# The MLP's second map for both token blocks at once: 26 block products added up in PSUM, with the sums for them made beside the first map

## The chip, the cores and the metric

The kernel runs on one core of a Trainium2 chip. The metric is the device time of one execution in microseconds (us), from the first instruction to the last. Engines named below: TensorE (PE, matmuls; PEld is its weight load), VectorE (DVE), ScalarE (ACT), GpSimd (POOL) and SyncE (SP). Here POOL does little besides issuing DMAs, and SP nothing else. SBUF is the on-chip memory of 128 partitions, PSUM the accumulator that TensorE writes: 8 banks of 128x512 floats. DRAM tiles are scratch outside the core.

## The reference

One layer over S = 2048 tokens of width D = 1024 in float32, with a conditioning vector that gives shift, scale and gate to each of two sub-layers. Cut to what matters:

```
mod = silu(c) @ w_ada + b_ada ; sh1, sc1, g1, sh2, sc2, g2 = split(mod)

h = x * (1 + sc1) + sh1 ; z = h @ w_in                    # 1024 -> 2048
mix = concat(gated conv of width 3, multi-scale pooling) @ w_out
x = LayerNorm(alpha * x + (1 + g1) * mix)

h = x * (1 + sc2) + sh2
f = square(relu(h @ w_mlp_in)) @ w_mlp_out                # 1024 -> 4096 -> 1024
x = LayerNorm(alpha * x + (1 + g2) * f)
```

The two matmuls of the last part, the first map (1024 to 4096) and the second map (4096 to 1024), are most of the arithmetic. Call U = square(relu(..)), 2048 x 4096, the first map's output, and W the second map's weights, 4096 x 1024.

## The kernel before, in words

*Precision.* TensorE multiplies a rounded float32 form at full speed. Each operand of a product is split in two: ScalarE casts it to a high part, VectorE subtracts that from the operand for a low part (`split`, L87 to L89; `parts` calls it for weights). A product is three matmuls, high times high, high times low, low times high (`mm3`, L92 to L95), so each operand tile of 128x1024 costs one cast on ScalarE and one subtraction on VectorE before TensorE may use it.

*Block products.* The tokens are two blocks b of T = 1024. The FF width is cut into NC = 8 column groups g of 512. Each matrix product is a 2x2 by 2x2 product in the form of Strassen and Winograd: 7 block products in place of 8, on sums of quarter blocks of each factor. Sums are VectorE adds (`tt`, L97), made once and kept in DRAM where more than one use needs them.

*Order of the stages.* For each token block: input projection, convolution and pooling, output projection, LayerNorm and transposes into blocks of the first map's token operand (`turned` with `back`; four sums pass through the DRAM tile `hsave`, L811), the first map, the second map, LayerNorm and store (`Close`). The first map, `up(b, g, B)` (L991), runs its 7 products for each g, 24 matmuls of 128x512 each, 56 products for a block; ScalarE does relu and square; VectorE makes sums of quarter blocks of U; POOL stores 8 tiles of 512 KB for each g in `usum` (`save`, L1012). Operand "4" of `back` is the last that column group 0 needs.

The weights' sums for the first map are made by `block_weights` (L518) as each g comes, or read back from `w1sum` for g below 2. The weights' sums for the second map are made by `sum_blocks` (L960) beside the first map of block 0: for each g and column half four loads of 256 KB on SP (L965), four adds of 128x512 and four stores on POOL (L971) to `w2sum`, with two fresh tiles each time.

The second map, `down(b, F, g2, close)` (L1116), runs once for each block. It has 7 products in 2 halves of 4 column groups; operands of the next half are loaded and split while this one is multiplied. Results are added from PSUM into eight row tiles F. In block 1 one of the seven products is cut once more (`DEEPER`, `deep_operands`, `deep_matmuls`, `deep_sums`): 7 products of quarter size, 8 x 7 x 6 = 336 matmuls of 128x256 in place of two halves of full size; its sums come from `sum_deep` (L974) and `closed` (L1062). `sum_x`, the gate's part of `ada` and `row_by_dram` (which turns the gate to a row) run beside the second map of block 0, as do `residual` (alpha times x in 8 rows) and `close.turn()`, which prepares the input projection of block 1.

*What sets the order.* The Python code names the work; a scheduler at build time lays the instructions of each engine down in one fixed order and hands out the slots of the tile pools: 28 tiles h, 10 o, 6 w, 5 r of 128x1024 floats, and 8 PSUM banks. An engine takes its instructions in that order and waits at each for its data and its tile. DMAs issued by SP and POOL stand in these engines' order too.

Of the kernel before, what the change touches and what calls it, by code (L numbers as in the profile page):

```python
# [13 lines left out]
P = 128  # L14
D = 1024
# [16 lines left out]
DEEPER = (1,)  # L32

DIRECT = 12
DEEP_SUMS = (0,), (1,), (2,), (3,), (4, 5), (6, 7), (), ()
HALF_SUMS = (1, 2, 3, 3, 3, 3, 3, 0)
# [14 lines left out]
def tile_hybrid_layer(ctx: ExitStack, tc: tile.TileContext, opening, xT, x, wada, win,  # L51
# [129 lines left out]
    w2sum = tc.dram_tile([NC, 4, P, T], F32, name="w2sum")  # L181
    usum = tc.dram_tile([NC, 8, P, T], F32, name="usum")
    hsave = tc.dram_tile([4, P, T], F32, name="hsave")
    nsave = tc.dram_tile([8, P, D], F32, name="nsave")
    rsave = tc.dram_tile([8, P, D], F32, name="rsave")
    gout = tc.dram_tile([2, KD // 2, P, T], F32, name="gout")
    winsum = tc.dram_tile([4, P, T], F32, name="winsum")
    w1sum = tc.dram_tile([2, 4, P, T], F32, name="w1sum")
# [4 lines left out]
    udeep = tc.dram_tile([NC, P, 3 * Q], F32, name="udeep")  # L193
    wdeep = tc.dram_tile([NC, P, T + 3 * Q], F32, name="wdeep")
# [323 lines left out]
    def block_weights(src):  # L518
        a11, a12, a21, a22 = [t_r() for _ in range(4)]
        for i, r in enumerate((a11, a12, a21, a22)):  # L520
            nc.sync.dma_start(r, src[i])
        yield a11
        yield a12
        s1 = t_r()
        tt(s1, a21, a22, ALU.add)
        tt(a21, a11, a21, ALU.subtract)
        tt(a11, s1, a11, ALU.subtract)
        tt(a12, a12, a11, ALU.subtract)
        for r in (a11, s1, a21, a12, a22):
            yield r  # L530
# [58 lines left out]
    def sum_x(k, after):  # L589
        ab = []  # L590
        for i in (k, k + 4):
            r = t_o()
            nc.sync.dma_start(r, xT[i])
            with tc.issue_after(after[0]):
                nc.scalar.activation(r, r, AF.Identity, bias=mod[:, 2 * i + SH1 : 2 * i + SH1 + 1],
                                     scale=mod[:, 2 * i + SC1 : 2 * i + SC1 + 1])
            ab += [r[:, :H], r[:, H:], r]
        b11, b12, b1, b21, b22, b2 = ab
        with tc.issue_after(after[1]):
            tt(b12, b12, b11, ALU.subtract)  # L600
# [265 lines left out]
    def out_proj(b, ops):  # L866
# [35 lines left out]
        def scale():  # L902
            t = late.pop()
            begun[:] = [nc.vector.tensor_scalar(R[t], R[t], mv[t][:, 0:1], mv[t][:, 6:7], op0=ALU.add,
                                                op1=ALU.mult).ins]
            nc.gpsimd.dma_start(nsave[t], R[t])
# [67 lines left out]
    def sum_deep(g):  # L974
        a, e = t_o(T), t_o(T)
        nc.sync.dma_start(a, w2[g, 2])
        b11, b12, b21, b22 = (a[:, i * Q : i * Q + Q] for i in range(4))
        t2, t3, t4 = (e[:, i * Q : i * Q + Q] for i in range(3))
        tt(t3, b22, b12, ALU.subtract)
        tt(b12, b12, b11, ALU.subtract)  # L980
        tt(t2, b22, b12, ALU.subtract)
        tt(t4, b21, t2, ALU.subtract)
        nc.gpsimd.dma_start(wdeep[g][:, :T], a)
        nc.gpsimd.dma_start(wdeep[g][:, T:], e[:, : 3 * Q])

# [3 lines left out]
    left = []  # L989

    def up(b, g, B):  # L991
        X, Y, Z = {}, {}, {}
        order = (0, 1, 5, 4, 6, 7, 3) if g else (0, 1, 7, 4, 5, 6, 3)
        product = seven(summed_weights(w1[g], w1sum[g], order) if g < 2 else block_weights(w1[g]), B)
        ps = [slice(p * H, p * H + H) for p in range(2)]

# [10 lines left out]
        def join(r, banks):  # L1007
            add(r, banks)
            nc.scalar.activation(r, r, AF.Relu)
            nc.scalar.activation(r, r, AF.Square)  # L1010

        def save(r, i):  # L1012
            nc.gpsimd.dma_start(usum[g, i], r)  # L1013

        product(0, X, True)
        c11 = keep(X)
        product(1, Y, True)
        join(c11, Y)
        save(c11, 0)
# [13 lines left out]
        else:  # L1033
            product(3, Z, True)
            c22 = keep(Z)
        product(4, X, False)
        join(c22, X)
        save(c22, 3)
# [5 lines left out]
        s1 = t_o()  # L1044
        tt(s1, c12, c22, ALU.add)
        tt(c12, c11, c12, ALU.subtract)
        tt(c11, s1, c11, ALU.subtract)
        for i, r in ((4, s1), (6, c12), (5, c11)):
            save(r, i)
# [5 lines left out]
        if b not in DEEPER:  # L1055
            tt(c11, c21, c11, ALU.subtract)
            save(c11, 7)
            save(c21, 1)
            return


        def closed(s4):  # L1062
            tt(s4, c21, c11, ALU.subtract)
            save(s4, 7)
            e = t_o()
            a11, a21, a12, a22 = (c21[:, i * Q : i * Q + Q] for i in range(4))
            q1, q2, q4 = (e[:, i * Q : i * Q + Q] for i in range(3))
            tt(q1, a21, a22, ALU.add)
            tt(q2, q1, a11, ALU.subtract)
            tt(a21, a11, a21, ALU.subtract)  # L1070
            tt(q4, a12, q2, ALU.subtract)
            save(c21, 1)
            nc.gpsimd.dma_start(udeep[g], e[:, : 3 * Q])

        if g + 1 < NC:
            closed(c11)
        else:
            left.append(closed)


    def down_operands(i, gs, scale=None):
        a, w = ORDER[i]
        out_ = []
        for g in gs:
            r = t_r()
            nc.sync.dma_start(r, usum[g, 3 + int(a[1]) if a[0] == "s" else 2 * int(a[0]) + int(a[1]) - 3])
            q = t_w(F32)
            nc.sync.dma_start(q, w2sum[g, int(w) - 1] if len(w) == 1 else w2[g, 2 * int(w[0]) + int(w[1]) - 3])
            if scale is not None:
                for hs in halves:  # L1090
                    tt(q[:, hs], q[:, hs], scale, ALU.mult)
            pair = []
            for src in (r, q):
                hi, lo = t_h(), t_h()
                done = split(src, hi, lo)
                pair += [hi, lo]
            out_.append(pair)
        return out_, done

    def residual():  # L1100
        ag, ab = row(t_o(D), rows[0]), row(t_o(D), rows[1])
        after = yield
        with tc.issue_after(after[0]):
            nc.scalar.mul(ag, ag, ALPHA)
        nc.scalar.mul(ab, ab, ALPHA)
        for t in range(8):
# [8 lines left out]

    def down(b, F, g2, close):  # L1116
        X, Y = {}, {}
        lo_, hi_ = halves
        closing = b + 1 == NB
        deeper = b in DEEPER  # L1120
        steps = [(i, hf) for i in ((1, 0) if deeper else (0, 1)) + (2, 3, 5, 4, 6) for hf in range(2)]

        def operands(n):
            i, hf = steps[n]
            return down_operands(i, range(4 * hf, 4 * hf + 4), g2[:, lo_] if closing and n + 1 == len(steps) else None)


        def matmuls(banks, ops, new, begins, ends, then, by_tile):
            if new and begins:
                for t in range(4):  # L1130
                    banks[t] = t_ps()
            every = range(len(ops))
            for t, n in ([(t, n) for t in range(4) for n in every] if by_tile else
                         [(t, n) for n in every for t in range(4)]):
                uh, ul, wh, wl = ops[n]
                for p in range(2):
                    cs = slice(p * H + t * P, p * H + t * P + P)
                    ws_ = halves[p]
                    mm3(banks[t], uh[:, cs], ul[:, cs], wh[:, ws_], wl[:, ws_],
                        new and begins and n == p == 0, ends and n == len(ops) - 1 and p == 1, not new)  # L1140
                if ends and n == len(ops) - 1:
                    then(t, banks[t])

        def keep(t, cs, ps):
            nc.scalar.copy(F[t][:, cs], ps)

        def add(t, cs, ps):
            tt(F[t][:, cs], F[t][:, cs], ps, ALU.add)

        def gate(t, cs):  # L1150
            tt(F[t][:, cs], F[t][:, cs], g2[:, cs], ALU.mult)

        def first_row(t, ps):
            add(t, hi_, ps)
            r = t_r()
            nc.sync.dma_start(r, rsave[t])
            gate(t, slice(0, D))
            for hs in halves:
                close.add(t, hs, r[:, hs])
            close.normalise(t)  # L1160


        def saved(hs):
            out_ = []
            for i in range(2):
                r = t_r()
                nc.sync.dma_start(r.rearrange("p (a n) -> p a n", a=2),
                                  rsave[4 + 2 * i : 6 + 2 * i, :, hs].rearrange("a p n -> p a n"))
# [3 lines left out]
        rest = {}  # L1172

        def second_row(t, ps):
            add(t + 4, hi_, ps)
            gate(t + 4, hi_)
            close.add(t + 4, hi_, rest[4][t])
            close.first_half(t + 4, 1)

        def last(t, ps):  # L1180
            tt(F[t + 4][:, lo_], ps, g2[:, lo_], ALU.mult)
            close.add(t + 4, lo_, rest[6][t])
            close.normalise(t + 4)

        def gated_first(t, ps):
            tt(F[t + 4][:, lo_], ps, g2[:, lo_], ALU.mult)
            tt(F[t + 4][:, lo_], F[t + 4][:, lo_], rest[6][t], ALU.add)

        def last_half(ops):
            for t in range(4):
# [306 lines left out]
```

## Time and profile before

The kernel took 1735.1 us, the median of 3 runs (1734.13 to 1736.8). The profile is that of one execution on the one core.

| | |
|---|---|
| median of runs | 1735.1 us |
| profiled execution, first to last instruction (its span) | 1733.2 us; its time is recorded by this span |
| TensorE busy | 1723.5 us, 99%, 7855 instructions |
| VectorE busy | 1314.6 us, 76%, 1726 instructions |
| ScalarE busy | 868.1 us, 50% |
| GpSimd busy | 205.8 us, 12% |
| DMA | 465.24 MB, mean 268 GB/s |

How such a profile is read: the busy line gives each engine's busy time, its share of the span and the number of its instructions. The slices cut the span into 40 equal parts, one digit each, in tenths. The chain that ended last is followed back from the last instruction, at each step to what released it; its shares say which engine or transfer the time lies on. A group line gives line, engine, operation, output and inputs with their shapes, count, then busy time and mean nanoseconds of one, then the idle time of the engine before them and what ended it. A source view of a DMA line gives the durations of the issuing instruction, the first and last start, and the time from issue to landing (least, median, most). A window row gives, for a stretch, the busy time of each engine with its instruction count, the granted clock of TensorE, the share of the DMA engines, and GB/s.

### The profile page before, as it was taken

What the parts mean: (1) busy time and instruction counts of PE and PEld (TensorE: products, weight loads), DVE (VectorE), ACT (ScalarE), POOL (GpSimd) and SP (SyncE); (2) the same over time, 40 slices, a digit from 0 to 9 for tenths busy, and PEclk for the clock granted to TensorE, in tenths of its full rate; (3) what the DMA queues carried; (4) which work ended last, traced back from release to release, by engine and by line L of the source; (5) the groups of instructions that cost most, each with busy time, mean ns of one, the idle gap of its engine ahead of it and who ended that gap; (6) DMA issues with size and microseconds to landing.
All of it is one profiled execution on the core that took longest, in us unless ns stands there. A gap on an engine that the chain in (4) does not pass through costs nothing.

```text
span 1733.2 us, 21912 instructions
## 1 busy us (share of the span) xinstructions
PE 1723.5 (99%) x7855; PEld 1435.5 (83%) x7855; DVE 1314.6 (76%) x1726; ACT 868.1 (50%) x1172; POOL 205.8 (12%) x399
## 2 busy tenths in 40 slices
PE   9999999999999999999999999999999999999998
PEld 7888888888888888888888888888888889888887
DVE  8897798877777686669686789687566778665896
ACT  6323368554445554446573344775444567444451
POOL 0222220122322000100000000102111110000000
PEclk9999999999999999999999999999999999999999
DMA  9998877778888998887572366657545589777771
GB/s 387 345 337 319 302 267 269 267 262 325 311 326 319 381 418 332 291 286 284 196 271 76 110 219 219 230 185 282 215 179 222 197 290 418 294 273 249 267 264 50
DMA packets 142685, 465.24 MB, mean 268 GB/s; under 512 B 16488, under 2 KB 17008, under 8 KB 142576
## 3 DMA queue, kind: packets, MB, share of 16 engines
q1 hardware_dynamic: 97920, 303.39, 48.0%
q0 software_dynamic: 44656, 160.46, 24.4%
q8 instruction: 61, 1.00, 0.2%
q14 instruction: 48, 0.39, 0.1%
HBM read 318.55 MB, written 145.23 MB: 268 GB/s over the span
## 4 chain that ended last, share of the span: by engine, by line
PE 95%; DMA 3%; issue 1%; DVE 1%; ACT 0%; SPq 0%; POOL 0%; DVEq 0%; POOLq 0%
PE ps L95 30%; PE ps L93 30%; PE ps L94 30%; PE ps L425 3%; DMA r<-in_w 1%; DMA usum<-o 1%; PE ps L773 1%; DVE o L98 0%; DMA o<-in_w 0%; DMA o<-in_opening 0%; DVE w L89 0%; DVE r L98 0%; ACT w L88 0%; DVE o L1369 0%; SPq L108 0%
## 5 line engine op out<-in xcount | busy, mean ns | idle before, releaser
L95 PE MATMUL ps<-h,w 128*128 128x512 f32 x1312 | 510.2, 389 | 0.4 <-DVE w L89 0.4
L94 PE MATMUL ps<-h,w 128*128 128x512 f32 x1312 | 510.3, 389 | 0.0
L93 PE MATMUL ps<-h,w 128*128 128x512 f32 x1312 | 510.0, 389 | 0.0
L93 PE MATMUL ps<-h,h 128*128 128x512 f32 (+1 forms) x1176 | 444.2, 378 | 0.0
L95 PE MATMUL ps<-h,h 128*128 128x512 f32 (+1 forms) x1176 | 444.1, 378 | 0.0
L94 PE MATMUL ps<-h,h 128*128 128x512 f32 (+1 forms) x1176 | 444.0, 378 | 0.0
L88 ACT CAST h<-r 128x1024 fp32r<-128x1024 f32 (+2 forms) x186 | 187.8, 1014 | 298.0 <-PE ps L94 186.8
L95 PEld LDWEIGHTS ps<-h,w 128*128 128x128 f32 x1312 | 246.3, 188 | 52.1 <-DVE w L89 0.8
L94 PEld LDWEIGHTS ps<-h,w 128*128 128x128 f32 x1312 | 246.3, 188 | 51.5 <-DVE h L89 0.5
L93 PEld LDWEIGHTS ps<-h,w 128*128 128x128 f32 x1312 | 246.0, 188 | 51.3 <-ACT h L88 0.2
L89 DVE TENSOR_TENSOR h<-r,h 128x1024 fp32r<-128x1024 f32 (+2 forms) x186 | 217.3, 1173 | 93.5 <-ACT h L88 93.0
L88 ACT CAST w<-r 128x1024 fp32r<-128x1024 f32 x156 | 164.3, 1053 | 242.6 <-PE ps L94 231.3
L89 DVE TENSOR_TENSOR w<-r,w 128x1024 fp32r<-128x1024 f32 x156 | 190.5, 1222 | 96.3 <-ACT w L88 95.4
L94 PEld LDWEIGHTS ps<-h,h 128*128 128x128 f32 x1176 | 221.3, 188 | 41.1
L95 PEld LDWEIGHTS ps<-h,h 128*128 128x128 f32 x1176 | 221.3, 188 | 40.8
L93 PEld LDWEIGHTS ps<-h,h 128*128 128x128 f32 x1176 | 221.3, 188 | 40.5
L98 DVE TENSOR_TENSOR o<-o,o 128x1024 f32<-128x1024 f32 (+2 forms) x193 | 171.1, 890 | 41.0 <-DMA usum<-o 31.8
L98 DVE TENSOR_TENSOR o<-o,ps 128x512 f32<-128x512 f32 (+1 forms) x175 | 113.7, 658 | 54.3 <-PE ps L95 53.4
L89 DVE TENSOR_TENSOR h<-w,h 128x1024 fp32r<-128x1024 f32 x114 | 137.6, 1207 | 4.3 <-ACT h L88 4.1
L88 ACT CAST h<-w 128x1024 fp32r<-128x1024 f32 x114 | 118.6, 1040 | 12.8 <-DMA w<-wdeep 4.1
L1013 POOL DMA_DIRECT2D usum<-o x111 | 59.4, 535 | 472.3 <-ACT o L1010 195.0
L98 DVE TENSOR_TENSOR r<-r,r 128x1024 f32<-128x1024 f32 x60 | 73.4, 1223 | 21.5 <-DMA r<-in_w 17.5
(160 smaller groups left out, 1243.0 us busy)
## 6 DMA issues: line engine op xcount, KB each, us to landing
usum<-o POOLq DMA_DIRECT2D x111, 512.0 KB, 4.8
r<-usum SPq DMA_DIRECT2D x109, 512.0 KB, 5.5
w<-w2sum SPq DMA_DIRECT2D x64, 512.0 KB, 5.9
r<-in_w SPq DMA_DIRECT2D x60, 512.0 KB, 6.0
w<-in_w SPq DMA_DIRECT2D x40, 512.0 KB, 7.4
o<-in_w SPq DMA_DIRECT2D x72, 256.0 KB, 6.4
w2sum<-o POOLq DMA_DIRECT2D x64, 256.0 KB, 6.7
msum<-o POOLq DMA_DIRECT2D x18, 512.0 KB, 4.9
```

The lines of the kernel that those rows point to most:

```text
L88: high = nc.scalar.copy(hi, src)
L89: return high.ins, nc.vector.tensor_tensor(lo, src, hi.bitcast(F32), op=ALU.subtract).ins
L93: nc.tensor.matmul(ps, whi, xhi, start=first, stop=False, skip_group_check=goes_on)
L94: nc.tensor.matmul(ps, whi, xlo, start=False, stop=False, skip_group_check=goes_on)
L95: nc.tensor.matmul(ps, wlo, xhi, start=False, stop=last, skip_group_check=goes_on)
L98: return nc.vector.tensor_tensor(out_, a, b_, op=op)
L425: nc.tensor.matmul(ps[m, h], wt[:, w : w + P], A[k][p // 2][:, hs], start=k == 0 and p == 0, stop=k == KD - 1 and p == 2)
L773: nc.tensor.transpose(ps[:, t * P : t * P + P], R[4 * h + t][:, k * P : k * P + P], ident)
L1013: nc.gpsimd.dma_start(usum[g, i], r)
```

## The change

The second maps of both token blocks become one stage behind both first maps. U is cut 4 by 4 (rows: each part holds a quarter of either block, 512 tokens together; columns: each part gathers 128 columns of every column group, 1024 together), W 4 by 2, and their product is formed from 26 block products (`PRODUCTS`), where the form of 7 for 2x2 by 2x2 would give 28. An entry of `PRODUCTS` names the sum of U, the sum of W, a sign, whether it starts a fresh set of PSUM banks, and which parts of the result read the banks behind it, with which factor. The products go by turns to two sets of 4 banks; one that is not fresh adds onto what its set already holds, so that sums of products are formed in PSUM. There are 8 fresh starts and 30 reads of a set into the 16 row tiles F. The stage is a stream of 26 x 4 units of 24 matmuls of 128x512, with operands loaded and split 4 units ahead. A negative sign is put into the split (in `operand`).

`up` makes 33 sums of 128x256 for each g and block in four stages (`U_SUMS`), and stores 26 tiles of 128 KB on POOL. `sum_down` makes the sums of W: for each of 8 column groups 13 loads, 20 adds of 128x512 (`W_SUMS`) and 17 stores, in four registers (halves of two tiles). It is a generator, drawn on by `beside()` at seven places of each column group of the first map (four in group 0): first the gate's part of `ada`, then 6 sums of W for each `sum_x`, the gate's row and the sums of the input weights, then 2 sums of W at each place, on through the first map of block 1. `block_weights` stores the first map's weight sums in block 0 for all g, and block 1 reads them back. `prepare` runs after the first map of block 0. `Close` serves 16 rows at once, and the output is stored by SP. The quarter-size stage and its sums are gone.

The diff, cut to its core (the tables of `U_SUMS`, `W_SUMS` and `PRODUCTS` with their first rows):

```diff
-DEEPER = (1,)
...
+SLOTS = 26
+RAW_SLOT = (0, 4)
+U_SUMS = (
+    ((1, 5, -1, 1, 16), (0, 1, 1, 2, 1), (16, 0, 1, 3, 19)),
...
+W_SUMS = (
+    (3, 6),
+    (2, 7),
+    (1, 3, 2, -1, 8),
+    (0, 4),
+    (2, 0, 3, -1, 9),
+    (0, 2),
+    (3, 0, 3, -1, 10),
+    (3, 1, 0, -1, 11),
...
+PRODUCTS = (
+    (13, 2, 1, True, ((3, 0, 1), (3, 1, 1))),
+    (2, 3, 1, True, ((0, 1, 1),)),
+    (15, 11, 1, False, ((3, 1, -1),)),
...
-    def block_weights(src):
+    def block_weights(src, dst=None):
...
+        if dst is not None:
+            for i, r in enumerate((s1, a11, a21, a12)):
+                nc.gpsimd.dma_start(dst[i], r)
...
-    def up(b, g, B):
+    def up(b, g, B, beside):
...
+        def stored(slot, z):
+            nc.gpsimd.dma_start(usum[slot, g // 2, :, b, g % 2, :], z)
+
+        def sums(stage):
+            if stage == 0:
+                stored(RAW_SLOT[0], parts_[RAW_SLOT[1]])
+            for x, y, sign, slot, at in U_SUMS[stage]:
...
+                z = parts_[at]
+                tt(z, where[x], where[y], ALU.add if sign > 0 else ALU.subtract)
...
+                if slot >= 0:
+                    stored(slot, z)
...
+    def sum_down():
+        for g in range(NC):
+            tiles = [t_o() for _ in range(2)]
+            regs = [r[:, hs] for r in tiles for hs in halves]
+            for step in W_SUMS:
+                if len(step) == 2:
+                    to, i = step
+                    src = w2[i, g // 2] if i < 8 else wsum[i - 8, g // 2]
+                    nc.sync.dma_start(regs[to], src[:, halves[g % 2]])
+                    continue
+                yield
+                to, x, y, sign, i = step
+                tt(regs[to], regs[x], regs[y], ALU.add if sign > 0 else ALU.subtract)
+                if i >= 0:
+                    nc.gpsimd.dma_start(wsum[i - 8, g // 2][:, halves[g % 2]], regs[to])
...
+    def down(g2, close):
...
+        def operand(n, gp):
+            s, w, sign = PRODUCTS[n][:3]
+            r = t_r()
+            nc.sync.dma_start(r, usum[s, gp].rearrange("p b g n -> p (b g n)"))
+            q = t_w(F32)
+            nc.sync.dma_start(q, w2[w, gp] if w < 8 else wsum[w - 8, gp])
...
+            hi, lo = t_h(), t_h()
+            if sign > 0:
+                split(r, hi, lo)
+            else:
+                nc.scalar.mul(hi, r, -1.0)
+                nc.vector.scalar_tensor_tensor(lo, r, -1.0, hi.bitcast(F32), op0=ALU.mult, op1=ALU.subtract)
+            return hi, lo, *parts(q)
...
+        stream = [(n, gp) for n in range(last + 1) for gp in range(4)]
+        ready = [operand(*x) for x in stream[:4]]
...
+            if k + 4 < len(stream):
+                ready.append(operand(*stream[k + 4]))
+            ops = ready.pop(0)
+            _, _, _, new, reads = PRODUCTS[n]
+            if gp == 0:
+                if new:
+                    banks[n % 2] = [t_ps() for _ in range(4)]
...
+            for i in range(4):
+                unit(banks[n % 2][i], i, ops, new and gp == 0, gp == 3, not new)
+            if gp == 3:
+                for t, d, c in reads:
+                    read(t, d, c, banks[n % 2])
...
-                store = nc.gpsimd if b + 1 < NB else nc.sync
-                store.dma_start(out[b * T + t * P : b * T + t * P + P, cs], z[:, cs])
+                nc.sync.dma_start(out[t * P : t * P + P, cs], z[:, cs])
...
+    def first_side():
+        for n in range(0, 8, 2):
+            ada(G2 + n, G2 + n + 2, nc.sync.dma_start, lambda: t_o(D))
+            yield
+        weights = sums_down
+        for n in range(4):
+            for _ in range(3):
+                next(weights)
+                next(weights)
+                yield
+            sum_x(n)
+            yield
...
+    def second_side():
+        for _ in sums_down:
+            next(sums_down, None)
+            yield
...
     for b in range(NB):
         B, back = out_proj(b, in_proj_1(*ready) if b else in_proj_0())
-        ready, gate = mlp(b, B, back, gate)
+        first_map(b, B, back)
+        if b == 0:
+            ready = prepare()
+    for _ in sums_down:
+        pass
+    close = Close()
+    down(gate[0], close)
```

494 lines of the change are left out of this document (200 added, 294 removed), and 3 rows, old and new, of the table U_SUMS.

## The prediction

> **What bounds the kernel now.** I read the page first: busy times, slices, and the chain that ended last.
>
> ```profile
> span 1733.2 us, 21912 instructions
> ...
> PE 1723.5 (99%) x7855; PEld 1435.5 (83%) x7855; DVE 1314.6 (76%) x1726; ACT 868.1 (50%) x1172; POOL 205.8 (12%) x399
> ...
> PE   9999999999999999999999999999999999999998
> ...
> PEclk9999999999999999999999999999999999999999
> ...
> PE 95%; DMA 3%; issue 1%; DVE 1%; ACT 0%; SPq 0%; POOL 0%; DVEq 0%; POOLq 0%
> ```
>
> TensorE is busy 99% of the span and is 95% of the chain: the kernel ends when its matmuls are done. So matmuls taken out pay at full price, and anything new that makes TensorE wait also does. The second view is the table of windows: a stretch of the first map of block 0, both first maps nearly whole, and the stage of quarter-size products that opens the second map of block 1.
>
> ```profile
> core 0: us, PE busy (x) PEld busy (x) DVE busy (x) ACT busy (x) POOL busy (x), PEclk, DMA share, GB/s
> 300.00:345.40 45.40, 45.40 (x201) 37.23 (x200) 38.15 (x40) 26.23 (x31) 5.89 (x11) 1.00 0.74 265
> 275.00:560.00 285.00, 284.57 (x1272) 235.44 (x1271) 221.35 (x249) 149.44 (x183) 67.09 (x125) 1.00 0.80 296
> 1121.00:1425.00 304.00, 304.00 (x1362) 252.00 (x1361) 217.08 (x255) 166.87 (x204) 42.31 (x79) 1.00 0.62 225
> 1424.31:1464.58 40.27, 40.27 (x337) 40.25 (x336) 33.27 (x37) 27.79 (x33) 2.67 (x5) 1.00 1.02 408
> ```
>
> Row one gives the pitch: 45.40/200 = 0.227 us a matmul of 512 columns, so a product of 24 takes 5.45. Rows two and three show how full the first maps are: VectorE 221 of 285 and 217 of 304, with TensorE full. VectorE's slack there, 64 and 87 us, is what the change draws on.
>
> **The change, part by part.** *Matmuls.* Before, the second map has 13 full block products of 8 groups times 24 matmuls (2496) and the quarter-size stage of 336 narrow ones. After, it has 26 products over 4 units of 24: 2496 again. So exactly the quarter-size stage goes, 40.27 us by row four: **−40.3**.
>
> *Durations for what is added* (VectorE, ScalarE and POOL groups by shape; busy time and mean ns stand behind the count):
>
> ```profile
> L89 DVE TENSOR_TENSOR w<-r,w 128x1024 fp32r<-128x1024 f32 x156 | 190.5, 1222 | 96.3 <-ACT w L88 95.4
> L98 DVE TENSOR_TENSOR o<-o 128x512 f32<-128x512 f32 x64 | 42.9, 686 | 4.7 <-DMA o<-gout 4.5
> L98 DVE TENSOR_TENSOR o<-o 128x256 f32<-128x256 f32 x40 | 15.9, 419 | 1.1 <-DMA o<-in_w 0.6 <-ACT o L1054 0.3
> L88 ACT CAST w<-r 128x1024 fp32r<-128x1024 f32 x156 | 164.3, 1053 | 242.6 <-PE ps L94 231.3 <-DMA o<-gout 4.7 <-DMA r<-in_wins 3.4
> ...
> L1013 POOL DMA_DIRECT2D usum<-o x111 | 59.4, 535 | 472.3 <-ACT o L1010 195.0 <-DVE o L98 176.8 <-DVE r L98 53.7
> ```
>
> *U sums.* Each column group and block makes 33 sums of 256 columns, 13.8 us by 0.419 (264 in block 0, 111 us), where it had 4 of 1024 columns (32×1.22 = 39): 72 us more for VectorE, which had 64 free. Stores to usum go from 111 to 416, 305×0.535 = 163 us more issue on POOL over two first maps; POOL was busy 67 of 285, so that fits.
>
> *W sums.* In place of 64 sums over four independent registers a half come 8 column groups of 20 sums of 512 columns, 13 loads (SP) and 17 stores (POOL), all in four half-tiles that are used again and again. A register may be loaded again only when its store has landed, and summed only when its load has landed. Followed sum by sum, 10 loads and 9 stores of a group stand one behind the other. With l and s for their times to landing, a group takes C = 10 l + 9 s + 20×0.685 (13.7). The source views of the like transfers of 256 KB, of 512 KB stores before that stage, and of the block loads:
>
> ```profile
> L965 SPq DMA_DIRECT2D o<-in_w x64: 327/424/1590, 320.7 to 545.9; - x64
> ...
> DMA to landing us min/median/max: 2.8/6.4/8.8
> ```
> ```profile
> L971 POOL DMA_DIRECT2D w2sum<-o x64: 542/542/552, 329.6 to 557.6; - x64
> ...
> DMA to landing us min/median/max: 3.6/6.5/9.1
> ```
> ```profile
> L545 POOL DMA_DIRECT2D w1sum<-w x8: 542/547/547, 241.5 to 255.8; - x8
> ...
> DMA to landing us min/median/max: 2.3/7.1/9.5
> ```
> ```profile
> L811 SPq DMA_DIRECT2D o<-hsave x4: 382/402/427, 308.0 to 1154.7; - x4
> ...
> DMA to landing us min/median/max: 4.2/5.2/7.0
> ```
>
> So l lies between 2.8 and 6.4 and s between 2.3 and 6.5. C is 28+21+13.7 = 62 at least and 64+58+13.7 = 136 at most.
>
> *Where the first group stands: a hole.* In the built order, the 20 sums of column group 0 are a nearly solid run on VectorE, right in front of the subtractions whose output is operand "4" of column group 0. These subtractions read blocks loaded back from hsave; those loads stand on SP behind the run's weight loads, and take the tile slots that the run frees. TensorE needs operand "4" for the last product of column group 0, after 10 products and the transposes of that map. So TensorE stops there, about 327 us into the span (the map begins near 269), until the run is through, and all behind the run on VectorE and SP waits with it. The run cannot start early: its second sum stands behind a split whose tile is freed by the product just before the stop. The stop is: cast and split 1.05+1.22; 10 loads and 9 stores; 19×0.685 = 13.0; the last store; the hsave load; sum, cast and split again (3.5). Little else is under way in a stop, so I take both l and s at 3.3, between the shortest seen and the medians and near the shortest: 2.3+62.7+13.0+3.3+4.2+3.5 = **+89**. At the shortest values 2.3+28+20.7+13+2.3+4.2+3.5 = 74; at the medians, with hsave 5.2, 153.
>
> By the Trainium skill ("DMA: Bandwidth & Descriptors", Anatomy of one DMA — SWDGE (gpsimd) path) such a transfer costs about 2.0 us plus its bytes over 436e3, an estimate of 2.6 us for 256 KB; the stop would be 2.3+49.4+13+2.6+4.2+3.5 = 75, and a group 63. The rows agree at their minimum, not at their median of 6.4.
>
> *Just behind the stop* VectorE has 67.5 us of its own work to 60 of TensorE's: **+6** (0 to 15).
>
> *Groups 1 to 3, first map of block 0.* They lie over the next 34 products, 185 us. Each starts when the one before has made 15, then 12, of its 20 sums, so they take 1+14/19+12/19 = 2.37 C. VectorE is in order: where a sum waits, the splits behind it wait too, and TensorE has operands for a few products only. VectorE's other work there is 58×1.22+42×0.685+177×0.42 = 174 us, which fills the waits in part; I take a quarter, 44, as not fitting. Transfers overlap with those of the stage, so l and s are halfway between shortest and median, 4.6 and 4.4: C = 46+39.6+13.7 = 99. 2.37×99+44 = 279, against 185: **+94**. From 0 (C = 62: 192, all but hidden) to 182 (C = 136).
>
> That such waits reach TensorE's chain at all is seen in the map before, where a loaded sum, a store and a reload stand in a row (the chain around 450 us; start, us, what):
>
> ```profile
> 444.14 9.05 DMA r<-in_w
> ...
> 459.35 0.54 POOL usum L1013
> 459.89 4.38 issue
> 464.28 3.85 DMA usum<-o
> 468.16 0.70 DVE o L98
> ...
> 508.21 7.72 DMA o<-in_w
> 515.98 1.86 DVE o L98 x3
> ```
>
> *Groups 5 to 7, first map of block 1*: 35.5 products, 193 us; 2.26 C; other VectorE work 137, a quarter 34. 2.26×99+34 = 258: **+65** (0 to 148).
>
> *Group 4* runs over from one block into the next, beside the input projection: **+5** (0 to 30).
>
> *Second map.* 26×96×0.227 = 567 us, operands asked for 4 units (21.8 us) ahead against 6.4 for a load; sums go from PSUM into F beside it, and VectorE, with two splits of 1.22 to each unit of 5.45 and 30 reads of 4 banks (82 us at 0.685), has a third of its time left. The out stores move from POOL to SP, in front of operand loads that have that lead. **0** (−15 to +15); with the lead gone, each late unit would cost its load, 6. *Moved work* (ada for the gate, xsum, the gate's row) goes into the first map of block 0: about 21 us of VectorE, counted in the 174 above. The stored w1 sums save 24 sums of 1.22 in block 1, which is in the 137. The residual and the input projection's preparation are the same work at another place: nothing, beside a full TensorE.
>
> *Sum.* 1735.1 − 40.3 + 89 + 6 + 94 + 65 + 5 = **1954**. All durations are from an execution of span 1733.2, 1.9 below the median, which I leave in. Ends: 1735.1−40.3+74−15 = 1754 and 1735.1−40.3+153+15+182+148+30+15 = 2238.
>
> **The rivals.**
> *Only the stop.* The later groups hide behind TensorE, if transfers land near their shortest time: 1735.1−40.3+89+6 = **1790**. For it: C = 62 gives 192 against 185. Against: in the loaded map the median load was 6.4.
>
> *The matmuls slow down after stalls.* In the start-up, small matmuls between waits are longer than the same in the filled stage:
>
> ```profile
> L127 PE MATMUL ps<-o 128*128 128x128 f32 x10 | 2.5, 437 | 1.1 <-DVE o L129 1.1
> L773 PE MATMUL ps<-ident,o 128*128 128x128 f32 x128 | 15.6, 275 | 0.0
> ```
>
> 437/275 = 1.59. If stalls brought that back all through the paced stages, they would be limited by TensorE itself: 34×5.45×1.59 = 295 for 279 and 35.5×5.45×1.59 = 308 for 258: 1954+66 = **2020**. Against: the clock row has no slice below 9, but also no long gap in it. By the Trainium skill ("TensorE: Matmul & The Clock Gate", Part 1: The HAM clock gate) the clock halves after an idle window of about 3.4 us and needs about as long busy to come back; products at twice their time would make 371 and 387, and 2175. No run so far shows such a gap.
>
> *The other side: faster.* The stop doesn't hold TensorE, and the groups pass behind it: 1735.1−40.3 = **1695**. The one mechanism is the run of group 0 being through before TensorE needs operand "4". It decides when the stop is under 40.3 us, that is (40.3−2.3−13.0−4.2−3.5)/20 = 0.9 us for each of the 20 transfers in its sum, or when the run begins 49 us sooner. The shortest transfer seen is 2.3.
>
> **How the numbers follow.** The forecast 0.60, with its own range 1840 to 2060 (a C of about 80 to 115 for both maps); only the stop 0.20; slow matmuls 0.10; faster 0.08; within 0.2%, which is what a measurement here can tell from no change, 0.02. Slower is thus 0.90. The range has to take in the stop alone (1790) and reach past the slow matmuls, and so runs from 1780 to 2150; the case of 1695, and what lies above, are left out.
>
> **What would show it.** A gap of TensorE of some 90 us from about 327 us on, ended by VectorE behind a load of hsave; in it, stores to wsum and loads of in_w of 256 KB by turns, and VectorE's waits put down to them. The first maps, 56 products or 305 us of matmuls each, at about 305+89+6+94 and 305+65. A second map of about 567 us with TensorE full, and no narrow matmuls at its start. If the granted clock falls below 1.00 around the gaps, the slow-matmul rival is right. The prediction is wrong if VectorE's waits in the later groups are short (transfers near 3 us, or groups that overlap more than 2.37 C says), or if the second map is short of operands.

## The result and the profile after

The changed kernel took 1978.6 us (median of 4 runs, 1976.97 to 1987.07) beside 1735.95 for the kernel before (median of 4): a ratio of 1.1407, interval 1.1383 to 1.1432. It is 14% slower. The forecast was 1954, with a range of 1780 to 2150.

The page of the changed kernel (span; busy line; slices of TensorE, VectorE and the granted clock; the chain that ended last):

```profile
span 1975.1 us, 22593 instructions
...
PE 1741.5 (88%) x7519; PEld 1422.8 (72%) x7519; DVE 1422.5 (72%) x2222; ACT 839.7 (43%) x1148; POOL 402.2 (20%) x767
...
PE   9999986218968875899998889789999999999998
...
DVE  7987867327767676688967667667666487686998
...
PEclk9999997659988988999999898989999999999999
...
PE 41%; issue 11%; DMA 11%; DVE 6%; POOL 3%; ACT 1%; DVEq 0%; SPq 0%; POOLq 0%; ACTq 0%
```

TensorE's work was to shrink by 40 us, yet its busy time rose from 1723.5 to 1741.5, and it now idles 234 us. The holes in its row begin in the sixth slice (from 247 us) and end with the 27th (1333 us); behind it the row is full. The clock row, without a digit below 9 before, goes down to 5 where TensorE stands still, and to 8 in many slices behind.

The windows table, cut at the first matmul of each stage, says where the time went. First the changed kernel: first map of block 0, input and output projection of block 1, first map of block 1, the joint second map.

```profile
core 0: us, PE busy (x) PEld busy (x) DVE busy (x) ACT busy (x) POOL busy (x), PEclk, DMA share, GB/s
269.70:762.50 492.80, 340.38 (x1379) 271.10 (x1379) 308.53 (x526) 181.72 (x233) 159.01 (x298) 0.83 0.66 223
762.50:1025.80 263.30, 236.87 (x1042) 194.21 (x1041) 207.50 (x294) 119.61 (x176) 39.10 (x70) 0.95 0.60 210
1025.80:1399.50 373.70, 329.69 (x1378) 265.84 (x1377) 249.44 (x451) 166.64 (x213) 132.37 (x248) 0.93 0.69 225
1399.50:1967.40 567.90, 566.49 (x2521) 469.65 (x2519) 425.22 (x537) 254.95 (x348) 16.84 (x32) 1.00 0.72 252
```

The same stages of the kernel before; here the second map of block 0 stands second and that of block 1 last:

```profile
269.40:578.60 309.20, 308.77 (x1378) 255.50 (x1377) 235.40 (x272) 165.72 (x213) 68.17 (x127) 1.00 0.81 299
578.60:883.30 304.70, 304.70 (x1346) 252.25 (x1345) 221.94 (x262) 161.02 (x207) 15.48 (x29) 1.00 0.82 305
883.30:1115.60 232.30, 232.29 (x1041) 192.48 (x1040) 182.22 (x250) 114.96 (x180) 17.80 (x30) 1.00 0.50 178
1115.60:1424.20 308.60, 308.60 (x1379) 255.66 (x1378) 220.98 (x267) 171.56 (x219) 42.34 (x79) 1.00 0.62 226
1424.20:1725.70 301.50, 301.50 (x1512) 257.58 (x1511) 222.14 (x264) 138.06 (x176) 6.95 (x13) 1.00 0.71 264
```

The second maps went from 304.7+301.5 = 606.2 to 567.9, a gain of 38.3. The first map of block 0 lost 183.6, the projections of block 1 lost 31.0, the first map of block 1 lost 65.1. The sum is +241.4, and the spans differ by 241.9.

*The stop.* VectorE's timeline in it (start, us, engine, line, operation, count, idle time before it and what ended that):

```profile
377.65 0.69 DVE L167 TENSOR_TENSOR o<-o,o 128x512 f32<-128x512 f32 x1 [3.01 <-DMA o<-in_w]
381.02 0.69 DVE L167 TENSOR_TENSOR o<-o 128x512 f32<-128x512 f32 x1 [2.68 <-DMA wsum<-o]
384.36 0.69 DVE L167 TENSOR_TENSOR o<-o,o 128x512 f32<-128x512 f32 x1 [2.64 <-DMA o<-in_w]
387.73 0.69 DVE L167 TENSOR_TENSOR o<-o,o 128x512 f32<-128x512 f32 x1 [2.67 <-DMA wsum<-o]
393.83 0.69 DVE L167 TENSOR_TENSOR o<-o 128x512 f32<-128x512 f32 x1 [5.41 <-DMA o<-in_w]
...
436.57 1.23 DVE L167 TENSOR_TENSOR o<-o,o 128x1024 f32<-128x1024 f32 x1 [4.23 <-DMA o<-hsave]
```

It is the run of sums of W that the prediction named, one sum of 0.69 and then a load or a store to wait for, by turns, and at its end the load of hsave. Where the wait is 5.4, a store and a load stand one behind the other. Over the whole first map of block 0 these are VectorE's two largest waits (us in total, times, longest):

```profile
DVE o L167 <- DMA o<-in_w: 82.7, 29, 5.4
DVE o L167 <- DMA wsum<-o: 26.5, 9, 6.4
```

The times to landing inside the stop, by the source views of the loads (L1153) and stores (L1159):

```profile
L1153 SPq DMA_DIRECT2D o<-in_w x11: 327/328/328, 361.8 to 428.4; - x11
...
DMA to landing us min/median/max: 2.5/2.6/4.6
```
```profile
L1159 POOL DMA_DIRECT2D wsum<-o x17: 540/540/543, 363.5 to 432.6; - x17
...
DMA to landing us min/median/max: 2.3/2.3/4.8
```

*After a stop the matmuls are slow.* TensorE's timeline at the end of the stop:

```profile
359.69 0.39 PE L164 MATMUL ps<-h,w 128*128 128x512 f32 x1
438.93 1.22 PE L162 MATMUL ps<-h,w 128*128 128x512 f32 x2 [78.85 <-ACT h L157]
440.19 0.79 PE L163 MATMUL ps<-h,w 128*128 128x512 f32 x1
440.78 0.63 PE L164 MATMUL ps<-h,w 128*128 128x512 f32 x1
441.20 0.63 PE L162 MATMUL ps<-h,w 128*128 128x512 f32 x1
441.63 0.63 PE L163 MATMUL ps<-h,w 128*128 128x512 f32 x1
...
445.16 0.39 PE L163 MATMUL ps<-h,w 128*128 128x512 f32 x1
445.38 0.39 PE L164 MATMUL ps<-h,w 128*128 128x512 f32 x1
```

The stop is 78.85 us. Behind it matmuls start 0.43 us apart and last 0.63, where elsewhere they start 0.227 apart and last 0.39; ten of them pass before the pitch is back. The granted clock in the windows around that place:

```profile
360.00:439.00 79.00, 0.15 (x2) 0.07 (x1) 17.16 (x26) 1.97 (x2) 10.89 (x21) 0.52 0.38 131
439.00:441.00 2.00, 1.96 (x4) 1.14 (x5) 1.47 (x2) 0.00 (x0) 0.00 (x0) 0.50 0.43 176
445.00:447.00 2.00, 2.00 (x11) 1.65 (x10) 0.00 (x0) 0.51 (x2) 0.00 (x0) 1.00 0.85 246
```

0.50 right behind the stop, 1.00 some six us later. From the first map on the changed kernel has 29 gaps of TensorE of 1 us or more, and nearly all of 2 us or more are followed by 7 to 15 such matmuls (or fewer, where the next gap comes first), some 1.5 to 3 us lost each time beside the gap itself. The total is read from the windows: TensorE was busy 340.38−308.77 + 236.87−232.29 + 329.69−308.60 = 57 us longer for the same instructions. So of the 280 us that the three stages lost, 222 are idle time and 57 longer busy time. Not all of the 57 is the clock: half of it was granted in 20 stretches of these stages, in which TensorE was busy for 95.9 us, and at a pitch of 0.427 for 0.227 about 45 of these are lost (an estimate). The other 12 were not taken apart; the last matmul before a gap counts with its whole 0.39 where one inside the stream adds 0.227, which is about 5 of them over 29 gaps. The Trainium skill ("TensorE: Matmul & The Clock Gate", Part 1: The HAM clock gate) has the clock at half after an idle window of about 3.4 us, and full again after about as long busy. The trace agrees on the half (0.50; 0.427/0.227 = 1.9) and on the few us; but a gap of 1.8 us, at 545 us, was already followed by nine slow matmuls, and so was one of the five gaps between 1.0 and 1.4 us (1.04, at 1104 us).

### The profile page after: what moved, and what is told of

The parts are those of the page before. It is cut to its first block, busy times and chain, and to the rows that moved or that the text cites. A ratio compares the mean times of both kernels' runs of the same rounds, so it can differ in the third digit from the quotient of the medians.

```text
span 1975.1 us, 22593 instructions
## 1 busy us (share of the span) xinstructions
PE 1741.5 (88%) x7519; PEld 1422.8 (72%) x7519; DVE 1422.5 (72%) x2222; ACT 839.7 (43%) x1148; POOL 402.2 (20%) x767
## 4 chain that ended last, share of the span: by engine, by line
PE 41%; issue 11%; DMA 11%; DVE 6%; POOL 3%; ACT 1%; DVEq 0%; SPq 0%; POOLq 0%; ACTq 0%
PE ps L163 14%; PE ps L164 14%; PE ps L162 13%; DVE o L167 4%; DMA o<-in_w 4%; DMA wsum<-o 3%; POOL usum L1080 2%; DMA usum<-o 2%; POOL wsum L1159 1%; DVE w L158 1%; DMA o<-hsave 1%; DVE r L167 0%; DMA xsum<-o 0%; DMA r<-usum 0%; PE ps L841 0%
## 5 line engine op out<-in xcount | busy, mean ns | idle before, releaser
L162 PE MATMUL ps<-h,w 128*128 128x512 f32 x1312 | 530.3, 405 | 145.7 <-ACT h L157 104.1
L164 PE MATMUL ps<-h,w 128*128 128x512 f32 x1312 | 527.4, 403 | 64.9 <-DVE w L158 64.8
L163 PE MATMUL ps<-h,w 128*128 128x512 f32 x1312 | 526.6, 401 | 3.0 <-DVE h L158 2.9
L163 PE MATMUL ps<-h,h 128*128 128x512 f32 (+1 forms) x1064 | 412.4, 388 | 0.9 <-DVE h L158 0.9
L162 PE MATMUL ps<-h,h 128*128 128x512 f32 (+1 forms) x1064 | 412.6, 388 | 0.5 <-ACT h L157 0.5
L164 PE MATMUL ps<-h,h 128*128 128x512 f32 (+1 forms) x1064 | 412.4, 388 | 0.0
L167 DVE TENSOR_TENSOR o<-o,o 128x256 f32<-128x256 f32 (+2 forms) x570 | 272.6, 520 | 153.6 <-DMA o<-in_w 108.0
L164 PEld LDWEIGHTS ps<-h,w 128*128 128x128 f32 x1312 | 255.6, 195 | 128.1 <-DVE w L158 73.9
L1080 POOL DMA_DIRECT2D usum<-o x416 | 222.4, 541 | 237.3 <-DVE o L167 164.7
L157 ACT CAST h<-r 128x1024 fp32r<-128x1024 f32 (+1 forms) x140 | 140.7, 1010 | 237.1 <-PE ps L163 109.6
L163 PEld LDWEIGHTS ps<-h,h 128*128 128x128 f32 x1064 | 199.8, 188 | 41.9 <-DVE h L158 1.3
L162 PEld LDWEIGHTS ps<-h,h 128*128 128x128 f32 x1064 | 199.8, 188 | 41.8 <-ACT h L157 0.9
L164 PEld LDWEIGHTS ps<-h,h 128*128 128x128 f32 x1064 | 199.8, 188 | 40.9
L158 DVE TENSOR_TENSOR h<-r,h 128x1024 fp32r<-128x1024 f32 (+1 forms) x140 | 162.6, 1167 | 62.5 <-ACT h L157 62.4
L167 DVE TENSOR_TENSOR o<-o 128x256 f32<-128x256 f32 (+1 forms) x224 | 118.9, 535 | 117.7 <-DMA o<-in_w 52.8
L1159 POOL DMA_DIRECT2D wsum<-o x136 | 73.5, 541 | 347.0 <-DVE o L167 335.7
L1067 ACT ACTIVATE o<-o 128x1024 f32<-128x1024 f32 x48 | 50.9, 1060 | 203.7 <-DVE o L167 203.6
```

The lines of the kernel that those rows point to most:

```text
L157: high = nc.scalar.copy(hi, src)
L158: return high.ins, nc.vector.tensor_tensor(lo, src, hi.bitcast(F32), op=ALU.subtract).ins
L162: nc.tensor.matmul(ps, whi, xhi, start=first, stop=False, skip_group_check=goes_on)
L163: nc.tensor.matmul(ps, whi, xlo, start=False, stop=False, skip_group_check=goes_on)
L164: nc.tensor.matmul(ps, wlo, xhi, start=False, stop=last, skip_group_check=goes_on)
L167: return nc.vector.tensor_tensor(out_, a, b_, op=op)
```

## The experiments

Every experiment is timed beside the kernel before on its own chip (1734.3 to 1735.1 us). Column group n stands for its seven products; in the kernel before, group 0 with the transposes takes 41.7 us from first matmul to first matmul, the others 38.1.

**1. The sums of W begin later.** The sums of W leave the place between the sum_x, and begin when those and the rest of the list are through:

```diff
-        weights = sums_down
         for n in range(4):
-            for _ in range(3):
-                next(weights)
-                next(weights)
-                yield
             sum_x(n)
             yield
```

> The sums of W begin only once the gate's part of ada, the four sum_x, the gate's row and the input weights' sums are through, so no register tile of theirs is freed into the slots that the loads of hsave take for operand "4". Nothing is left out. Theory (the stop and the later waits are chains of transfers): the stop of 79 us and the slow matmuls behind it (some 3 us) go, the later groups still wait: 1880 to 1905. Rival (VectorE is simply full of sums in the first maps, and the stop only shows it): the same sums still have to pass, so most of the time comes back behind: 1930 to 1980.

Measured: 1930.8 us (ratio 1.1133, 1.1116 to 1.1149), 48 below the changed kernel. The stop of 78.9 is gone; in its place stand gaps of 21.2, 8.1 and 10.8 us, behind the sum_x that moved up. So the stop came from where that run stood, but the time was only in part to be had: by the number, the rival, at the very edge of its range.

**2. Registers loaded once.** The sums are all made, on whatever the registers hold:

```diff
+            for i, r in enumerate(regs):
+                nc.sync.dma_start(r, w2[i, g // 2][:, halves[g % 2]])
             for step in W_SUMS:
                 if len(step) == 2:
...
-                    nc.sync.dma_start(regs[to], src[:, halves[g % 2]])
                     continue
...
-                if i >= 0:
-                    nc.gpsimd.dma_start(wsum[i - 8, g // 2][:, halves[g % 2]], regs[to])
```

> Each column group of W loads its four registers once, at its start, and then makes all 20 sums; the other 9 loads and all 17 stores are left out, and the second map reads raw blocks of W in place of the sums, so the output is not the reference's. VectorE has as many sums as before. Theory (chains of transfers): the stop shrinks to one load, the 20 sums and the load of hsave, about 27 us, and nearly all later waits go: 1710 to 1770. Rival (VectorE full): the sums are all there, so only the stop's 50 us go: 1900 to 1930.

Measured: 1826.4 us (1.0530, 1.0515 to 1.0546). The stop was 27.5 us, as expected. The whole lies between the two theories.

**3. No sums of W.** `sum_down` only yields.

> The sums of W are left out, with their loads and stores; the second map reads raw blocks of W, so the output is not the reference's. All sums of U stay. If the sums of W are the whole cause, the first maps are back at the 309 us they took in the kernel before and the time is 1695 to 1710. If the 33 sums of U for each group (72 us more on VectorE) hold TensorE up by themselves, it is above 1730.

Measured: 1788.8 us (1.0317, 1.0301 to 1.0332). So the sums of W cost 1978.6−1788.8 = 190 us in this order of the work; by run 2, 152 of them hang on their transfers and 38 on the sums. But 54 us above the kernel before remain without them, 93 above what the second map's gain alone would give: the forecast had no such part. Column groups 0 to 2 of block 0 took 74.2, 47.5 and 47.9 us, groups 0 and 1 of block 1 53.0 and 47.5, the projections of block 1 242.8 against 232.3. VectorE's timeline of this run at the start of the first map shows one cause:

```profile
285.02 1.23 DVE L278 SCALAR_TENSOR_TENSOR o<-o,o 128x1024 f32<-128x1024 f32 x1 [5.54 <-DMA o<-in_wada]
287.50 1.23 DVE L278 SCALAR_TENSOR_TENSOR o<-o,o 128x1024 f32<-128x1024 f32 x1 [1.25 <-DMA o<-in_wada]
...
296.50 1.23 DVE L278 SCALAR_TENSOR_TENSOR o<-o,o 128x1024 f32<-128x1024 f32 x1 [2.34 <-DMA o<-in_wada]
...
323.16 1.23 DVE L278 SCALAR_TENSOR_TENSOR o<-o,o 128x1024 f32<-128x1024 f32 x1 [4.84 <-DMA o<-in_wada]
...
327.62 2.49 DVE L167 TENSOR_TENSOR o<-o,o 128x1024 f32<-128x1024 f32 x2 [3.03 <-DMA o<-hsave]
```

The moved `ada` waits for its own loads, in VectorE's order, ahead of the operands that the transposes make; TensorE stands still for 7.1, 1.5 and 14.9 us there, in the changed kernel too (6.5, 1.5, 15.0).

**4. No sums of U.**

```diff
-                if at not in parts_:
+                if False:
...
-                z = parts_[at]
-                tt(z, where[x], where[y], ALU.add if sign > 0 else ALU.subtract)
+                z = where[x]
```

> The 33 sums of U for each group are left out; the 26 stores stay and store unsummed cells, so the output is not the reference's. VectorE loses 111 us of work in each first map; the sums of W stay with all their transfers. Theory (chains of transfers): the stop stays at about 79 us, the later waits shrink a little since VectorE catches up between them: 1860 to 1930. Rival (VectorE full): with 220 us less work nearly all of the loss but the stop goes: 1760 to 1800.

Measured: 1854.1 us (1.0698, 1.0680 to 1.0715), between the theories and just outside the first. The run can't tell them apart: the edit also drops the sums' three tiles, and the 79 us stop is gone from it (no gap in that map above 7.1). That the slots fall otherwise without these tiles is likely, but not shown. What the run does show is the start of each map. In block 0, with `ada` where it was, TensorE's gaps in group 0 were 4.3, 1.1 and 5.6 us, and the group took 59.0 where the changed kernel takes 73.9. In block 1 groups 0 and 1 took 41.7 and 38.3, as before the change, with all sums of W made. So what these groups lost in run 3 comes from the sums of U, by their time or their tiles: in block 1 all of it, in block 0 together with `ada`.

**5 and 6. A quiet start**, without and with the sums of W. Nothing is drawn beside the map until operand "4" is made; the gate's part of `ada` moves to block 1; sums of U made before that point are held back:

```diff
         def beside():
-            next(side, None)
+            if on:
+                next(side, None)
...
+        on.append(1)
+        while held:
+            held.pop(0)()
         for g in range(NC):
             for _ in ups[g]:
```

> As the run without sums of W (1788.8 us), and the start of each first map is cleared: nothing is drawn beside it until operand "4" is made, the gate's part of ada and the gate's row move to the first map of block 1 behind that point, and the sums of U of the first two column groups are held back until there. The sums of W are left out and the second map reads raw blocks, so the output is not the reference's. Theory (what is left without W is VectorE waiting for ada's loads and making sums of U ahead of the operands): the 52 us that column groups 0 to 2 of block 0 and the 20 us that groups 0 and 1 of block 1 lie above the kernel before mostly go: 1715 to 1740. Rival (VectorE has too much to do in the first map of block 0, wherever it stands): 1770 to 1790.

> The run with late sums of W (1930.8 us), and the same clearing of the start of each first map. Nothing is left out. Theory: the early waits go in both maps, some 45 to 70 us, and the waits of the sums of W stay: 1860 to 1890. Rival (the work only meets the sums of W later): 1915 to 1935.

Measured: 1757.8 us (1.0131, 1.0116 to 1.0146) without the sums of W, 1884.8 (1.0847, 1.0820 to 1.0874) with them. Both gain, 31 and 46 us; the second is within its theory, the first between theory and rival. Group 0 of both blocks is back at 41.7. Without W, groups 1 and 2 still took 49.3 and 63.0: ScalarE stood 13.8 us at the loads of sum_x, and waited for tiles.

**7. The sum_x spread as well**, without the sums of W:

```diff
+        for _ in range(8):
+            yield
         for n in range(4):
             sum_x(n)
-            yield
+            for _ in range(7):
+                yield
```

> The cleared start without sums of W (1757.8 us), where TensorE still stands 7.8 and 22.1 us in column groups 1 and 2 of block 0 while ScalarE waits for the loads of sum_x and for tiles. Here the four sum_x are drawn one at a time, one column group apart, from group 2 on. The sums of W are left out and the second map reads raw blocks, so the output is not the reference's. Theory (it is the four sum_x close together, with ScalarE in order at their loads): both waits go with their slow matmuls, about 35 us: 1718 to 1732, below the kernel before. Rival (the held-back sums of U of the first groups need that time on VectorE): 1745 to 1760.

Measured: 1733.4 us (0.9987, 0.9975 to 0.9998). The mechanism was the theory's: both waits went, and groups 1 and 2 took 38.3 each. The gain was 24 us where about 35 were expected, and the time lies 1.4 above the theory's range; the projections of block 1 took 6.4 us more than in run 5. So what the run without W had lost hung on the order of work that is the same in amount: the moved steps, which wait for loads at the head of an in-order engine, and the sums of U of the first groups. Run 5 moves `ada` and these sums in one edit and doesn't part them. And this is what the 26 products are worth when the sums of W cost nothing: the kernel before, within 0.2%. The gain of the second map (570.1 us here against 606.2) is still paid for elsewhere: the first maps at 316.0 and 321.5, 6.8 and 12.9 above before, and the projections of block 1 at 250.3, 18.0 above.

**8. The same with all sums of W**, six ahead of each sum_x.

> The cleared start with all sums of W (1884.8 us), with six sums of W ahead of each sum_x, so that the sum_x are spread. Nothing is left out. Theory: the 29 us of the two early waits go, and the sums of W cost what they cost there otherwise, some 125 us above the run without them: 1840 to 1865. Rival (TensorE's waits only change places, since VectorE has no time to spare once the sums of W wait for their transfers): 1875 to 1895.

Measured: 1888.0 us (1.0880, 1.0859 to 1.0901): the rival. TensorE's early waits came back as others, and the sums of W cost 1888.0−1733.4 = 155 us. The same sums cost 190 in the changed kernel and 127 between runs 5 and 6, so their price depends on what else stands in VectorE's order. VectorE's waits in the first map of block 0 of that run:

```profile
DVE o L167 <- DMA o<-in_w: 57.4, 27, 9.3
DVE o L167 <- DMA wsum<-o: 17.5, 7, 6.7
DVE w L158 <- ACT w L157: 15.0, 9, 5.2
```

**9 and 10. The chain on GpSimd.** Loads, adds and stores of W go to POOL's own queue, the stores of U to SP; 9 on the order of run 1, 10 on that of run 6.

```diff
-                    nc.sync.dma_start(regs[to], src[:, halves[g % 2]])
+                    nc.gpsimd.dma_start(regs[to], src[:, halves[g % 2]])
...
-                tt(regs[to], regs[x], regs[y], ALU.add if sign > 0 else ALU.subtract)
+                nc.gpsimd.tensor_tensor(regs[to], regs[x], regs[y], op=ALU.add if sign > 0 else ALU.subtract)
...
-            nc.gpsimd.dma_start(usum[slot, g // 2, :, b, g % 2, :], z)
+            nc.sync.dma_start(usum[slot, g // 2, :, b, g % 2, :], z)
```

> The run with late sums of W (1930.8 us), with each chain of W on GpSimd alone: its loads, its adds and its stores, in GpSimd's order; the stores of sums of U go from POOL to SP. Nothing is left out. Theory (a wait of the chain costs because VectorE stands still at it, with the splits behind): VectorE no longer waits for in_w or wsum, and the time comes near the run without sums of W: 1790 to 1850. Rival (the transfers themselves, or the tiles that the chain holds, keep TensorE waiting whichever engine adds): 1900 to 1960.

> Both edits: the cleared start and the sums of W on GpSimd. Nothing is left out. Theory: both causes go, 1715 to 1780; below 1735 it would beat the kernel before. Rival (the chain holds TensorE up by itself): above 1840.

Measured: 2092.8 us (1.2059, 1.2022 to 1.2097) and 1983.9 (1.1433, 1.1416 to 1.1450). Both went the rival's way; run 9 was 162 us slower than the same on VectorE, beyond either expectation. VectorE no longer waits for the sums' loads (o<-in_w) or for wsum in the first map of block 0. The group on GpSimd, then TensorE's and ScalarE's longest waits in that map (run 9):

```profile
L1157 POOL TENSOR_TENSOR o<-o,o 128x512 f32<-128x512 f32 x96 | 158.3, 1654 | 146.5 <-DMA o<-in_w 121.6 <-DMA wsum<-o 24.0
```
```profile
PE ps L162 <- ACT o L1055: 109.5, 9, 38.4
```
```profile
ACT o L1067 <- DVE o L167: 78.5, 20, 8.5
ACT o L1055 <- DMA usum<-o: 54.9, 5, 30.6
...
ACT o L1055 <- POOL o L1157: 15.4, 1, 15.4
```

A sum takes 1.65 us on GpSimd, 2.4 times VectorE's 0.69, and TensorE now waits for ScalarE at L1055, which copies a product out of PSUM and has no o tile to copy to: the ten tiles are held, by stores of U that stand in SP's order and by the chain. The wait moved from VectorE's queue to the pool and to SP. How it splits between the slower sums, the held tiles and SP's order was not taken apart.

## Why the prediction came out as it did

The total was close, 1954 forecast and 1978.6 measured, and the direction right. The mechanism of its two largest steps is the one that the runs show; that the total came so near is luck in part, since errors of both signs stand against each other. By its steps:

- **Matmuls, −40.3.** Right: −38.3, and the second map is full (566.5 of 567.9), 567 forecast. The last term, 0 for prefetch and out stores in the second map, held.
- **The stop, +89.** Right in its place in the order, its cause and its end; measured 78.9, and 3.3 of slow matmuls behind it. It began at 359.7 us and not at 327, since group 0 had lost 32 us ahead of it. The size was off in the landings: 3.3 each was taken, 2.6 for loads and 2.3 for stores measured. My reason, that little else is under way, was right (the DMA share was 0.38 there) and I should have gone by it to the shortest rows, which give 74. With 2.6 and 2.3 the same sum gives 72; the other 7 us stand in no term of it (VectorE waits 2.68 for a store that lands in 2.3). The estimate from the Trainium skill's "DMA: Bandwidth & Descriptors", Anatomy of one DMA — SWDGE (gpsimd) path, 2.6 us and 75 for the stop, was nearer than mine. The page gives it for DMAs issued by GpSimd, as the stores are; the prediction used it for the loads too, which SP issues. In this stop the trace is near it for both, and not over all groups, where the medians were 4.0 for the loads and 3.5 for the stores.
- **VectorE behind the stop, +6, and groups 1 to 3, +94.** Together 100; column groups 2 to 7 of block 0 took 298.4 us against 229.3, so +69, slow matmuls included. The mechanism is the one named: run 2, which takes most transfers away and leaves the sums, gains 152 of the 190 us. The landings were as taken (behind the stop the medians were 4.5 for loads and 4.2 for stores; 4.6 and 4.4 in the term). Too large was the part of the waits that no other work fills: the term leaves VectorE 279−174−2.37×13.7 = 73 us idle at them, and it stood 52.8 (its waits from 439 to 763 us):

```profile
DVE o L167 <- DMA o<-in_w: 40.8, 18, 4.8
...
DVE o L167 <- DMA wsum<-o: 12.0, 4, 6.4
```

- **Moved work, counted as 21 us of VectorE inside the 174.** Wrong, the step that failed most clearly. It was costed by its durations and not by its loads' waits, and group 0 has no term in the sum at all. TensorE stopped 23 us at the start of the map (group 0 took 73.9 for 41.7), where VectorE waits for the loads of `ada`, and the sum_x cost some 24 us where they stood together (run 5 against run 7). `ada` is not the whole of the first: without the sums of U (run 4) the stops there are 11 us.
- **Group 4, +5, and "preparation at another place: nothing".** Measured +31.0, just above the 0 to 30 given. Without any sums of W it is still +10.5 (run 3), so some 20 hang on the sums of W. Of the 10.5, a single gap of 6.2 us and the slow matmuls behind it are most; ahead of the split that ends this gap VectorE has no pause above 0.2 us from 634 to 651 us, with splits of the input projection's preparation and sums of U of the last column group. The preparation has lost the second map of block 0 as its cover, but how the gap divides between the two was not taken apart.
- **First map of block 1, +65.** Measured +65.1, by luck in part: about 20 of it, in groups 0 and 1, remain without the sums of W (run 3), and go without the sums of U (run 4). These two groups were to lose nothing.
- **Slow matmuls**, given as a rival at 0.10 and +66: they came, about 45 us of them, not in place of the stalls but on top of them, some ten after each stall. The sign given for this rival, a granted clock below 1.00 around the gaps, is there; that TensorE would be limited by them all through was wrong. The forecast proper had no term for them. So the total is near because the stop and the waits of groups 1 to 3 were taken too large, and the loss of group 0, most of that of the projections and the slow matmuls were left out.

*Only the stop* (1790) and *faster* (1695) fall: without the stop the time was 1930.8, and even with no sums of W at all 1733.4 was the best. No version run here is faster than the kernel before by more than 0.2%, complete or not. More tiles o, or more registers for each chain of W, were not tried.

## What to carry to other kernels

On an in-order engine, cost a step that waits for its own transfers by those waits and by what stands behind it in the queue, and not by its busy time: here 20 sums of 0.69 us stopped TensorE for 79. Before work is moved beside a full stage, list each of its loads and the tiles it holds there, since a tile freed late is a wait for whoever is handed its slot. And when matmuls are the bound, look for slow matmuls behind each stall: here a stall of a few us cost another 1.5 to 3 us, so many small stalls are dearer than their sum.

## What was not expected of the hardware

The clock: 0.50 granted right after a stall, and matmuls 0.427 us apart for 7 to 15 of them, after gaps as short as 1.8 us and once 1.04; about 45 us of the 242 lost. The half clock was granted in stretches of 3.41 us and multiples of it (6.83, 10.24, and 81.9 around the stop), and of the five gaps between 1.0 and 1.4 us four were followed by none and one by a whole stretch. GpSimd beside VectorE: in run 9 a sum of 128x512 took 1.56 to 1.65 us on GpSimd, and over the whole run the sums of 128x256 on VectorE took 0.465 us on average where they take 0.42, the splits into w 1.296 where they take 1.22. That the sums on GpSimd are what slows VectorE was not tested by itself.
